# A transformer block in one program: the order of TensorE's three-product steps and of some small products

## The chip, the cores and the metric

The program runs on one core of a Trainium2 chip. The metric is the device time of one execution in microseconds (us); the time given for a kernel is the median of several executions. A profile is one execution of its own, with a start and a duration for every instruction of TensorE (PE, matmuls; PEld, the loads of their stationary operands), VectorE (DVE), ScalarE (ACT), GpSimd (POOL) and SyncE (SP, which issues most transfers).

## What is computed

One block of a hybrid network on a sequence of 1024 positions with 1024 features, all float32. `h` is normalised and multiplied by one wide matrix; three kinds of mixing work on slices of the result, and a gated merge and a feed-forward part follow:

```python
h = _rms(x, norm_mix_g[i])
proj = h @ w_in[i]                                  # 1024 x 8224
p_nsa, p_rwkv, p_gdn, p_gate = jnp.split(proj, ...)
o_a = _nsa(...)      # attention: compressed, selected and window keys
o_b, v_first = _rwkv7(...)                          # a recurrence with 8 heads of 64
o_c = _gdn(...)      # gated delta rule in chunks, 4 heads of 128
merged = gate0 * (o_a @ w_branch0) + gate1 * (o_b @ w_branch1) + gate2 * (o_c @ w_branch2)
x = x + merged @ w_out[i]
h = _rms(x, norm_ffn_g[i])
x = x + jnp.square(jax.nn.relu(h @ w_ff1[i])) @ w_ff2[i]
```

## The kernel before

**Dense steps.** The five large matrix products (`w_in`, three times `w_branch`, `w_out`, `w_ff1`, `w_ff2`) are done in a split form. Each float32 operand is held as a high part and a low part (`split`, L256 on): ScalarE casts the raw tile to the high part (`whi`, L259), and GpSimd or VectorE subtracts it from the raw tile to get the low part (`wlo`, L264), so the low part of a weight is always written last. One dense step is then three products of 128x128 by 128x512 into the same PSUM tile `fps`: high by high, high by low, low by high. There are 2368 such steps (7104 products). `mm3_steps` holds the loop for `w_in`; `tail` holds four more copies of the three lines, one for each later matrix.

**Small steps.** The three mixings are chains of small products with VectorE, ScalarE and GpSimd between them. They write PSUM tiles named `mps`. Some fill the whole 128x128 array (transposes against `ident`; `gZ,KQ`; the products of `PH` and `PL`, the high and low part of attention weights, with `V2s` and `V2w`); others use only 64 or 32 of its rows or columns (`xs,U`, `VS,AG`, `wa,up`, and `PH` or `PL` with `V2c`, the compressed values, which have 64 rows). A row of the profile shows that as 128\*128, 64\*128 and so on.

**What sets the order.** The code is written as generators. `run` steps the small chains, and between them takes single dense steps (`dense_step`) as filler, a share of TensorE's time that `BESIDE`, `GBESIDE` and `NBESIDE` set. The order in which the instructions then stand on each engine is chosen when the program is built: every instruction carries a priority number, `tc.cur_priority` at the time it was written, and dense steps are written with a number raised by 78, 100 or 1000 (`self.delta`), so that small steps that are ready go first. The built order is fixed; on the chip each engine goes through its own list, and an instruction waits on semaphores for operands from other engines. Before the change each of the three products of a dense step is placed by itself.

**The stages**, by the time in the profile before: the norm and the first columns of `w_in` (0 to 150 us), the recurrence `rwkv` with filler (150 to 630), `gdn` with filler (630 to 1050), the preparation of attention (1050 to 1160), attention with filler, from the middle on the first half of the tail (1160 to 1700), then the rest of the tail, which is dense steps almost alone (1700 to the end, with a seam between its two halves from 2000 to 2137).

Weights of `w_in` come in tiles of 512 rows by 128 columns, with two buffers for the raw tile and two for the parts (`FRAW`, `FBUF`); their low part is made on GpSimd alone (`FDIV`).

## Time and profile before

| | |
|---|---|
| median of 3 executions | 2495.28 us (2484.92 to 2502.08) |
| profiled execution | 2491.57 us, of which span of the profile 2489.5 us |
| instructions | 37131, of them 13589 matmul records |
| TensorE busy | 2357.2 us (95% of the span) |
| VectorE, ScalarE, GpSimd busy | 1396.8, 1060.3, 965.8 us |
| mean granted clock of TensorE | 0.974 |

A matmul's busy time in the profile includes what overlaps with the next one: a dense product has a duration of 390 to 430 ns, and the next one starts 0.23 us after it. The cost of a product is therefore read from the distance between two starts, not from its duration. The granted clock is a share of 2.4 GHz; it has two levels here, 1.0 and 0.5.

### The profile page before, as it was taken

To read this page: it belongs to the slowest core of one execution; us is meant where nothing else is said; L and a number is where in the kernel's file an instruction comes from. 1 tells how busy PE (TensorE), PEld (TensorE's weight loads), DVE (VectorE), ACT (ScalarE), POOL (GpSimd) and SP (SyncE) were. 2 spreads that over 40 slices of the span, in tenths; PEclk is the share of its full clock that TensorE was granted. 3 is DMA by queue.
4 is the path that set the end of the run, shared out by engine and by line. 5 is a ranking of instruction groups with operands and counts; after the bars stand their busy time and mean duration, and the time that the engine had idled before them with its cause. 6 is when DMAs were issued, how large, how long until landed. Compare 5 with 4: busy or idle time off the path is not lost.

```text
span 2489.5 us, 37131 instructions
## 1 busy us (share of the span) xinstructions
PE 2357.2 (95%) x13589; PEld 1891.7 (76%) x13589; DVE 1396.8 (56%) x3139; ACT 1060.3 (43%) x2101; POOL 965.8 (39%) x967
## 2 busy tenths in 40 slices
PE   6989999999899899899999999899999989999999
PEld 4767777777777778687887778788888867788887
DVE  4366766662675765223557787775444446545444
ACT  5454443322443433235667675654323334423231
POOL 4434444333221211235446684353333346233332
PEclk9989899999999999899999999999999999999999
DMA  4222223222223212552214331014323354223232
GB/s 139 69 64 64 59 66 76 68 72 69 69 55 84 53 49 80 146 114 73 62 56 135 97 110 42 21 62 138 101 94 95 109 181 145 82 89 110 85 110 93
DMA packets 319718, 216.79 MB, mean 87 GB/s; under 512 B 78486, under 2 KB 273184, under 8 KB 319536
## 3 DMA queue, kind: packets, MB, share of 16 engines
q1 hardware_dynamic: 308672, 195.63, 27.5%
q10 hardware_dynamic: 9792, 17.83, 2.0%
q8 instruction: 107, 1.75, 0.3%
q0 software_dynamic: 1072, 0.96, 0.2%
q14 instruction: 75, 0.61, 0.1%
HBM read 178.16 MB, written 36.22 MB: 86 GB/s over the span
## 4 chain that ended last, share of the span: by engine, by line
PE 77%; DVE 10%; DMA 5%; ACT 4%; issue 2%; POOL 1%; SPq 1%; ACTq 0%; DVEq 0%; POOLq 0%
PE fps L97 57%; PE mps L97 16%; PE mps L101 4%; DVE inv_p L341 2%; DVE inv_u L343 1%; DMA cw<-in_nsa_cmp_w_dram 1%; DVE gacc L895 1%; DMA lb<-inv 1%; DMA wraw<-in_w_branch_dram 1%; ACT P L1362 1%; DMA inv<-LT 1%; DVE ast L1357 1%; POOL wlo L264 0%; ACT whi L259 0%; DVE ast L1360 0%
## 5 line engine op out<-in xcount | busy, mean ns | idle before, releaser
L264 POOL TENSOR_TENSOR wlo<-wraw,whi 128x512 fp32r<-128x512 f32 (+2 forms) x408 | 525.1, 1289 | 907.1 <-ACT whi L259 877.9
L259 ACT CAST whi<-wraw 128x512 fp32r<-128x512 f32 (+1 forms) x408 | 286.6, 704 | 635.9 <-PE fps L97 430.6
L97 PE MATMUL fps<-hTh,whi 128*128 128x512 f32 x1024 | 442.5, 434 | 10.5 <-DVE wa L439 7.5
L97 PE MATMUL fps<-hTl,whi 128*128 128x512 f32 x1024 | 414.8, 407 | 0.0
L97 PE MATMUL fps<-hTh,wlo 128*128 128x512 f32 x1024 | 413.3, 408 | 1.3 <-POOL wlo L264 1.2
L264 DVE TENSOR_TENSOR wlo<-wraw,whi 128x256 fp32r<-128x256 f32 (+1 forms) x207 | 131.5, 638 | 224.6 <-ACT whi L259 219.3
L97 PEld LDWEIGHTS fps<-hTh,whi 128*128 128x128 f32 x1024 | 198.9, 195 | 52.3 <-DVE wa L439 7.6
L97 PEld LDWEIGHTS fps<-hTh,wlo 128*128 128x128 f32 x1024 | 198.3, 194 | 47.2 <-POOL wlo L264 2.7
L97 PEld LDWEIGHTS fps<-hTl,whi 128*128 128x128 f32 x1024 | 199.7, 195 | 32.5 <-issue 0.3
L97 PE MATMUL fps<-h2h,whi 128*128 128x512 f32 x512 | 200.0, 391 | 1.3 <-DVE h2l L296 1.3
L1376 POOL TENSOR_SCALAR P<-P,ast 128x64 f32<-128x64 f32 (+5 forms) x128 | 137.9, 1094 | 161.6 <-DVE ast L1369 96.1
L97 PE MATMUL fps<-h2l,whi 128*128 128x512 f32 x512 | 199.5, 390 | 0.0
L97 PE MATMUL fps<-h2h,wlo 128*128 128x512 f32 x512 | 199.3, 390 | 0.0
L97 PE MATMUL fps<-whi,fl 128*128 128x512 f32 x512 | 191.0, 389 | 0.0
L97 PE MATMUL fps<-whi,fh 128*128 128x512 f32 x512 | 189.9, 391 | 0.0
L97 PE MATMUL fps<-wlo,fh 128*128 128x512 f32 x512 | 189.0, 389 | 0.0
L1455 DVE TENSOR_TENSOR acc<-fps,acc 128x512 f32<-128x512 f32 x160 | 106.8, 686 | 105.8 <-PE fps L97 105.5
L1362 ACT ACTIVATE P<-mps,ast 128x128 f32<-128x128 f32 (+4 forms) x256 | 125.1, 494 | 72.5 <-DVE ast L1360 42.4
L1357 DVE TENSOR_REDUCE ast<-mps 128x1 f32<-128x128 f32 (+4 forms) x256 | 109.0, 442 | 56.6 <-PE mps L97 53.8
L1405 DVE TENSOR_TENSOR PL<-mps,PH 128x512 fp32r<-128x512 f32 (+2 forms) x168 | 103.3, 620 | 48.8 <-ACT PH L1404 48.1
L1404 ACT CAST PH<-mps 128x512 fp32r<-128x512 f32 (+2 forms) x168 | 88.2, 534 | 64.9 <-PE mps L101 59.4
L97 PEld LDWEIGHTS fps<-h2h,whi 128*128 128x128 f32 x512 | 96.2, 188 | 21.4 <-DVE h2l L296 1.8
(468 smaller groups left out, 4696.6 us busy)
## 6 DMA issues: line engine op xcount, KB each, us to landing
wraw<-in_w_in_dram SPq DMA_DIRECT2D x152, 256.0 KB, 2.9
wraw<-in_w_ff_dram SPq DMA_DIRECT2D x128, 256.0 KB, 2.8
wraw<-in_w_ff_dram SPq DMA_DIRECT2D x64, 512.0 KB, 3.4
gates<-fst ACTq DMA_DIRECT2D x48, 256.0 KB, 2.0
wraw<-in_w_branch_dram SPq DMA_DIRECT2D x48, 256.0 KB, 3.1
gin<-gates SPq DMA_DIRECT2D x48, 256.0 KB, 3.0
wraw<-in_w_out_dram SPq DMA_DIRECT2D x16, 512.0 KB, 3.4
nsa_in<-fst ACTq DMA_DIRECT2D x20, 256.0 KB, 2.1
```

What stands on the lines that cost most here:

```text
L97: return self.note(self.nc.tensor.matmul(out, lhsT=lhsT, rhs=rhs, **kw))
L101: return self.note(self.nc.tensor.transpose(out, x, ident))
L259: nc.scalar.copy(hi, raw)
L264: eng.tensor_tensor(out=lo[:, x], in0=raw[:, x], in1=hi[:, x].bitcast(F32), op=OP.subtract)
L341: nc.vector.tensor_tensor(out=v, in0=lt[:n, s, None, s + 1:].to_broadcast([n, w, w]), in1=u[:n, s + 1:, s + 1:].rearrange("p t c -> p c t" ...
L343: nc.vector.tensor_reduce(out=u[:n, s, s + 1:], in_=v, axis=AX, op=OP.add)
L1357: nc.vector.tensor_reduce(out=(mx if i == 0 else mx2)[:, b:b + 1], in_=ps[:, :n], axis=AX, op=OP.max, negate=True)
L1362: nc.scalar.activation(out=Pt[:, c:c + n], in_=tiles[i][:, :n], func=AF.Exp, bias=mx[:, b:b + 1], accum_out=(sm if i == 0 else sm2)[:, b:b ...
L1376: eng.tensor_scalar(out=Pt[:, c:c + n], in0=Pt[:, c:c + n], scalar1=r[:, b:b + 1], scalar2=None, op0=OP.mult)
L1404: nc.scalar.copy(PH[:n, x0:x1], ps[:n, x0:x1])
L1405: tt(out=PL[:n, x0:x1], in0=ps[:n, x0:x1], in1=PH[:n, x0:x1].bitcast(F32), op=OP.subtract)
L1455: tt(out=acc[:, st, c0:c0 + 512], in0=ps, in1=acc[:, st, c0:c0 + 512], op=OP.add)
```

## The change

Two things change, both only on TensorE. First, a dense step is written by a new helper `three`: the product with the low part of the weights comes first, and the second and third are written with a priority number 4000 lower, so that they stand right behind the first. Second, in four places small products are written in another order: the one whose operand is written last comes first (`rk` before `sq`; the heads in reversed order in two loops of the recurrence; `PL` before `PH`). No product, operand or buffer is added or taken away.

```diff
@@ mm3_steps
-            self.te.matmul(ps, lhsT=wh[:, k, m], rhs=rh[:, kk, n], start=(kk == 0), stop=False)
-            self.te.matmul(ps, lhsT=wh[:, k, m], rhs=rl[:, kk, n], start=False, stop=False)
-            self.te.matmul(ps, lhsT=wl[:, k, m], rhs=rh[:, kk, n], start=False, stop=(kk == (kts or kt) - 1))
+            self.three(ps, (wl[:, k, m], rh[:, kk, n]), (wh[:, k, m], rh[:, kk, n]), (wh[:, k, m], rl[:, kk, n]),
+                       kk == 0, kk == (kts or kt) - 1)
             yield
+    def three(self, ps, a, b, c, start, stop):
+        self.te.matmul(ps, lhsT=a[0], rhs=a[1], start=start, stop=False)
+        at = self.tc.cur_priority
+        self.tc.cur_priority = max(0, at - 4000)
+        self.te.matmul(ps, lhsT=b[0], rhs=b[1], start=False, stop=False)
+        self.te.matmul(ps, lhsT=c[0], rhs=c[1], start=False, stop=stop)
+        self.tc.cur_priority = at
@@ _rwkv_unit
+            self.te.matmul(ps[:, 8 + 2 * i:10 + 2 * i], lhsT=rk[:, two], rhs=sums[:, 2 * pp + i // 2], start=True, stop=True)
             self.te.matmul(ps[:, 2 * i:2 * i + 2], lhsT=sq[:, two], rhs=sums[:, 4], start=True, stop=True)
-            self.te.matmul(ps[:, 8 + 2 * i:10 + 2 * i], lhsT=rk[:, two], rhs=sums[:, 2 * pp + i // 2], start=True, stop=True)
...
-            for x, h, o in heads:
+            for x, h, o in reversed(heads):
                 self.te.matmul(pv[o, 0, x], lhsT=ag[:, x, h], rhs=vs[:, x, h], start=True, stop=True)
...
-            for x, h, o in heads:
+            for x, h, o in reversed(heads):
                 self.te.matmul(pv[o, 2, x], lhsT=kb[:, x, h], rhs=vs[:, x, h], start=True, stop=True)
@@ _pv_mm
-            self.te.matmul(po, lhsT=v, rhs=PH[:n, x], start=(b0 + j == 0), stop=False)
-            self.te.matmul(po, lhsT=v, rhs=PL[:n, x], start=False, stop=(b0 + j == last))
+            self.te.matmul(po, lhsT=v, rhs=PL[:n, x], start=(b0 + j == 0), stop=False)
+            self.te.matmul(po, lhsT=v, rhs=PH[:n, x], start=False, stop=(b0 + j == last))
@@ tail (w_out and w_ff2; w_branch and w_ff1 in the same way)
-                        self.te.matmul(ps, lhsT=lhs[0](k0 + k)[:, m], rhs=wh[:, j, :], start=(k == 0), stop=False)
-                        self.te.matmul(ps, lhsT=lhs[0](k0 + k)[:, m], rhs=wl[:, j, :], start=False, stop=False)
-                        self.te.matmul(ps, lhsT=lhs[1](k0 + k)[:, m], rhs=wh[:, j, :], start=False, stop=(k == 3))
+                        hi, lo = (t(k0 + k)[:, m] for t in lhs)
+                        self.three(ps, (hi, wl[:, j, :]), (hi, wh[:, j, :]), (lo, wh[:, j, :]), k == 0, k == 3)
```

What that does to the built order shows at two places. The first is TensorE in attention, at its third unit of queries and heads (`ident,P` transposes the attention weights, `PH` and `PL` are their parts, `K2c` the compressed keys, `fps` a dense product). Before:

```order
L97 MATMUL mps<-PH,V2w 128x256
L97 MATMUL mps<-PL,V2w 128x256
L101 MATMUL mps<-ident,P 128x128 x4
L97 MATMUL fps<-hTh,whi 128x512
L97 MATMUL fps<-hTl,whi 128x512
L97 MATMUL fps<-hTh,wlo 128x512
L97 MATMUL mps<-PH,V2c 128x256
L97 MATMUL fps<-hTh,whi 128x512
L97 MATMUL mps<-PL,V2c 128x256
L101 MATMUL mps<-ident,P 128x128 x4
```

The same place in the changed kernel:

```order
L97 MATMUL mps<-K2c,QL 128x64
L97 LDWEIGHTS identb
L97 MATMUL mps<-mcmp,identb 128x64
L97 MATMUL fps<-hTh,wlo 128x512
L97 MATMUL fps<-hTh,whi 128x512
L97 MATMUL fps<-hTl,whi 128x512
L97 MATMUL mps<-PL,V2c 128x256
L97 MATMUL mps<-PH,V2c 128x256
L101 MATMUL mps<-ident,P 128x128 x4
```

The two products with `V2c` had a dense product between them and now stand together, behind a whole dense step.

The second place is TensorE early in the recurrence, where one PSUM tile of dense steps, `fps_561`, gives way to the next, `fps_660` (the names carry their buffer numbers here; `gd,upg` is a small product that fills the array). Before:

```order
L97 MATMUL fps_561<-hTh_132,wlo_595 128x512
L97 MATMUL fps_660<-hTh_132,whi_663 128x512
L97 MATMUL fps_660<-hTl_133,whi_663 128x512
L97 MATMUL mps_1853<-gd_490,upg_1670 128x256 x2
L97 MATMUL fps_660<-hTh_132,wlo_664 128x512
```

The same place in the changed kernel:

```order
L97 MATMUL fps_561<-hTh_132,wlo_595 128x512
L97 MATMUL fps_561<-hTh_132,whi_594 128x512
L97 MATMUL fps_561<-hTl_133,whi_594 128x512
L97 MATMUL mps_1853<-gd_490,upg_1670 128x256 x2
L97 MATMUL fps_660<-hTh_132,wlo_664 128x512
```

The small products stood between the second and the third product of the first step of `fps_660`; now they stand between two whole steps.

Counted over TensorE's whole list: of 2368 dense steps 175 had small products among their three before, and 12 have now; 284 had products of another dense step among them, and 44 have now. Small products come in 598 groups between dense products before, in 514 now. The part of the array that a product uses (128\*128, 64\*128, 128\*64, 64\*64, 32\*32) changes from one product to the next 706 times before, 618 times now. The two products of each `V2c` pair stand apart in 25 of 32 cases before, in none now. The first product of a dense step carries 481 semaphore waits before and 751 now, the second 183 and 246, the third 419 and 59; small products carry 1734 and 1666.

## Rows read from the trace of the kernel before

**Rows 1.** The page's busy times: busy us, share of span, count.

```profile
PE 2357.2 (95%) x13589; PEld 1891.7 (76%) x13589; DVE 1396.8 (56%) x3139; ACT 1060.3 (43%) x2101; POOL 965.8 (39%) x967
```

**Rows 2.** Windows by stage: stretch, length, busy us and count by engine, clock.

```profile
1160.00:1610.00 450.00, 432.49 (x2520) 353.22 (x2520) 310.56 (x748) 296.93 (x767) 252.76 (x212) 0.98 0.24 74
150.00:630.00 480.00, 460.11 (x3850) 345.11 (x3849) 285.44 (x799) 177.26 (x325) 181.47 (x218) 0.95 0.27 68
630.00:1050.00 420.00, 382.02 (x2264) 312.37 (x2262) 257.77 (x690) 156.87 (x260) 95.77 (x110) 0.96 0.27 74
...
1700.00:2000.00 300.00, 300.00 (x1335) 248.56 (x1333) 145.79 (x197) 95.64 (x144) 102.24 (x86) 1.00 0.33 108
```

**Rows 3.** The page's chain of waits that ended last, share by engine.

```profile
PE 77%; DVE 10%; DMA 5%; ACT 4%; issue 2%; POOL 1%; SPq 1%; ACTq 0%; DVEq 0%; POOLq 0%
```

**Rows 4.** Timeline of PE, attention: start, us, instruction; a pair apart.

```profile
1173.49 0.40 PE L97 MATMUL fps<-hTh,wlo 128*128 128x512 f32 x1
1173.81 0.38 PE L97 MATMUL mps<-PH,V2c 64*128 64x256 f32 x1
1174.12 0.50 PE L97 MATMUL fps<-hTh,whi 128*128 128x512 f32 x1
1174.56 0.38 PE L97 MATMUL mps<-PL,V2c 64*128 64x256 f32 x1
1174.87 0.66 PE L101 MATMUL mps<-ident,P 128*128 128x128 f32 x4
```

**Rows 5.** Timeline of PE, attention, a pair together.

```profile
1219.30 0.28 PE L97 MATMUL mps<-PH,V2w 128*128 128x256 f32 x1
1219.41 0.28 PE L97 MATMUL mps<-PL,V2w 128*128 128x256 f32 x1
1219.63 0.38 PE L97 MATMUL mps<-PH,V2c 64*128 64x256 f32 x1
1219.85 0.28 PE L97 MATMUL mps<-PL,V2c 64*128 64x256 f32 x1
1220.06 0.44 PE L101 MATMUL mps<-ident,P 128*128 128x128 f32 x2
```

**Rows 6.** Timeline of PE, recurrence: dense products behind small ones on part of the array.

```profile
406.94 0.45 PE L97 MATMUL mps<-xs,U 64*64 64x64 f32 x8
407.31 0.50 PE L97 MATMUL fps<-hTh,whi 128*128 128x512 f32 x1
407.65 0.39 PE L97 MATMUL fps<-hTl,whi 128*128 128x512 f32 x1
407.88 0.40 PE L97 MATMUL fps<-hTh,wlo 128*128 128x512 f32 x1
```

**Rows 7.** Timeline of PE, recurrence: a dense product before whole-array transposes.

```profile
164.58 0.39 PE L97 MATMUL fps<-hTh,wlo 128*128 128x512 f32 x1
164.81 0.60 PE L101 MATMUL mps<-ident,BK 128*128 128x128 f32 x4
```

**Rows 8.** PE's waits, 150 to 1700 us: waiter, awaited, us in total, times, longest.

```profile
PE mps L97 <- DVE VS L712: 7.8, 10, 2.1
PE mps L97 <- ACT P L1362: 7.6, 12, 1.7
```

**Rows 9.** PE's waits over the whole span; columns as in rows 8.

```profile
PE fps L97 <- ACT whi L259: 4.9, 5, 1.8
...
PE fps L97 <- POOL wlo L264: 1.2, 2, 0.6
```

**Rows 10.** Groups by form: busy us, mean ns, then idle us before and its releasers.

```profile
L264 POOL TENSOR_TENSOR wlo<-wraw,whi 128x512 fp32r<-128x512 f32 x257 | 366.5, 1427 | 594.0 <-ACT whi L259 575.1 <-PE mps L97 10.3 <-PE fps L97 4.6
L259 ACT CAST whi<-wraw 128x512 fp32r<-128x512 f32 x328 | 202.8, 620 | 516.7 <-PE fps L97 353.3 <-DMA wraw<-in_w_ff_dram 55.9 <-issue 36.1
```

**Rows 11.** Windows in late attention; columns as in rows 2, clock third from last.

```profile
1590.60:1600.80 10.20, 9.40 (x40) 8.51 (x41) 6.05 (x16) 10.03 (x23) 0.04 (x1) 0.50 0.03 7
1576.00:1590.60 14.60, 10.93 (x69) 8.50 (x67) 10.16 (x27) 11.05 (x27) 7.93 (x6) 1.00 0.13 37
```

More of the change, by code (lines that the diff above doesn't have):

```diff
@@ L1477, in tail @@
                             for k in range(4):
-                                self.te.matmul(ps, lhsT=wh[:, k], rhs=oh[k], start=(k == 0), stop=False)
-                                self.te.matmul(ps, lhsT=wh[:, k], rhs=ol[k], start=False, stop=False)
-                                self.te.matmul(ps, lhsT=wl[:, k], rhs=oh[k], start=False, stop=(k == 3))
+                                self.three(ps, (wl[:, k], oh[k]), (wh[:, k], oh[k]), (wh[:, k], ol[k]), k == 0, k == 3)
                                 yield
@@ L1509, in up @@
                                 k = kh * 4 + j
-                                self.te.matmul(ps, lhsT=wh[:, j], rhs=h2[0][:, k], start=(k == 0), stop=False)
-                                self.te.matmul(ps, lhsT=wh[:, j], rhs=h2[1][:, k], start=False, stop=False)
-                                self.te.matmul(ps, lhsT=wl[:, j], rhs=h2[0][:, k], start=False, stop=(k == KT - 1))
+                                self.three(ps, (wl[:, j], h2[0][:, k]), (wh[:, j], h2[0][:, k]), (wh[:, j], h2[1][:, k]),
+                                           k == 0, k == KT - 1)
                                 yield
```

## The prediction

> **What bounds the kernel now.** I read the busy times first, then the windows by stage, then the chain of waits, and last the timeline of TensorE at the places that the change touches. The busy times put TensorE far ahead: 2357.2 us of the 2489.5 us span [rows 1]. So 2489.5 - 2357.2 = 132.3 us of the span are open gaps on it. The windows say where: from 1700 to 2000 us there is no gap at all and the clock is at its upper level, 2.4 GHz; in the recurrence the gaps are 480 - 460.1 = 19.9 us, in `gdn` 420 - 382.0 = 38.0 us, in attention 450 - 432.5 = 17.5 us [rows 2], together 75.4 us. The chain that ended last agrees: 77% of it is TensorE, 10% VectorE [rows 3]. So the time is TensorE's own work plus its gaps, and a change that only moves TensorE's instructions can do three things: make the same work take less between two starts, close gaps, or open others. The dense tail, where nothing stands between dense steps, can give nothing: there one product follows another and no order of the three changes their number.
>
> A busy TensorE is read by distances between starts. A dense product behind a dense product takes 0.23 us (407.65 to 407.88) [rows 6].
>
> **The change part by part.**
>
> *Pairs with the compressed values.* A product that uses 64 of 128 rows costs more at its edges. In [rows 4] the dense product before `PH,V2c` lasts from 1173.49 to 1173.81, 0.32 us instead of 0.23; `PH,V2c` takes 0.31; the dense product between the two takes 0.44 (1174.12 to 1174.56); `PL,V2c` takes 0.31. From 1173.49 to 1174.87 that is 1.38 us, and without two dense products at 0.23 it is 0.92 us. Where the two stand together [rows 5], the product before them takes 0.22 instead of the 0.11 of its like, an extra of 0.11, and they take 0.22 and 0.21: 0.54 us. The difference is 0.38 us a pair, and 25 of 32 pairs are brought together. All 25 would give 9.5 us; where the neighbours of an apart pair are themselves on part of the array, one edge is saved instead of two, which I bound by half, 4.8 us. Most apart pairs stand between full-size products as in [rows 4], so I take 8 us.
>
> *Other edges.* The used part of the array changes 88 times less often. The 25 pairs hold two changes each, 50; 38 are left. An edge into part of the array costs 0.32 - 0.23 = 0.09 us (1173.49 to 1173.81) [rows 4], an edge back costs 0.34 - 0.23 = 0.11 us (407.31 to 407.65) [rows 6]. 38 x 0.10 = 3.8 us; bounds 3.4 and 4.2. The other groups that disappear go between full-size products, where the dense product before whole-array transposes takes its normal 0.23 us (164.58 to 164.81) [rows 7]: no price, so none of the 598 - 514 = 84 vanished groups is counted for itself.
>
> *Whole steps before small ones.* 175 - 12 = 163 dense steps no longer let small products in between their three. At each of these places one or two dense products, 0.23 or 0.45 us, now run before the small product, whose operands have that much longer to come. What TensorE waited there shrinks; what it did not wait is unchanged. The two largest kinds of waits of small products hold 22 waits and 15.4 us [rows 8]. If 175 of 598 groups, 0.29, hold the same share of waits, 6 of the 22 shrink by a mean 0.34 us, 2 us; scaled from 15.4 to the 75.4 us of gaps it is 10 us. But many other gaps are single waits at the start of a stage that no third of a microsecond closes, so I take 4 us, bounds 2 and 10.
>
> *The low part first.* The lead of a dense step now waits for `wlo`, which takes GpSimd 1.43 us behind the cast to `whi` [rows 10]; before, two products (0.45 us) ran in that time. Where TensorE already waited for `whi`, 5 times and 4.9 us in all [rows 9], the wait grows, by up to 5 x (1.43 - 0.45) = 4.9 us; the low end is 0, where a small step's end decides in any case. ScalarE, GpSimd and VectorE get no more to do, but the weight tile's high part is released one product (0.23 us) later and its low part is needed two products (0.45 us) earlier: the cycle of release, cast, subtraction and lead loses 0.68 us of slack at each load of `w_in`. It stays hidden as long as the load in the other buffer, at least twelve products or 2.7 us, outlasts cast and subtraction, 0.62 + 1.43 = 2.05 us [rows 10]. TensorE waited for `wlo` only 1.2 us in all [rows 9], so there is slack, thin where there is little small work. I take a loss of 3 us.
>
> *Reversed heads, `rk` before `sq`.* The same products on the same parts of the array; one wait on the last operand in place of two, the first of which ended while the second was still pending. I take 0; at most 0.1 us for each of 64 places in either direction if the chain through them ends last.
>
> *The clock.* From 1590.6 to 1600.8 us the granted clock was at 0.50, that is 1.2 GHz, although TensorE was busy for 9.40 of 10.2 us with transposes and small products; just before it had been at 2.4 GHz, with gaps of 14.60 - 10.93 = 3.7 us in the 14.6 us that went ahead [rows 11]. [...]
>
> The sum: -8 - 3.8 - 4 + 3 = -12.8 us on the profiled execution's 2491.57 us, 2478.8 us. That execution lay 3.7 us below the median 2495.28 us of the runs shown, so the forecast for a median is 2482 us, half a per cent faster. With all bounds at their ends it is -24 to -5 us, 2471 to 2490 us.
>
> **The rivals.**
>
> *The gaps close much more.* With whole steps as units the built order might fit the chip better everywhere. If a third of the 75.4 us of gaps went, 25 us, with the edges (12) and the loss (3), the change would be -34 us: 2461 us. For it: 163 places get more cover, and small products carry 68 semaphore waits less. Against it: the gaps that have names in [rows 8] are few, and the number of dense products between a small step's last link and its next looks much the same in both orders.
>
> *Small chains held back, the slower side.* In `gdn` and in the recurrence each link of a chain goes from TensorE to VectorE and back. A link that finds a dense step begun now waits 0.23 or 0.45 us. As long as filler is left, TensorE loses nothing, since it works in that time; from the point on where a stage ends with its chain and not with its filler, every such wait counts. `gdn` has the widest gaps, 38.0 us [rows 2], which speaks for it. 163 places x 0.34 us = 55 us if all of them were on the path; with half of them 28 - 12 + 3 = +19 us: 2514 us. Against it: 77% of the chain is TensorE's own work [rows 3], and 84 + 11 of the 175 places lie in attention and behind it, where two streams and the tail's filler stand in.
>
> *The clock.* If the longer stretches without dense products cost two more low stretches like that of [rows 11], each of 10.2 us at half the clock, 5 us apiece, the sum becomes -3 us: 2492 us.
>
> *The edges are worth nothing.* If a chain through the other engines ends each mixed stage, the 12 us saved on TensorE become wider gaps: 2494 us. Against it stands a TensorE that is 91 to 96% busy in these stages [rows 2].
>
> That the change does not do what it says is excluded by the built order: 2312 of 2368 steps stand whole, 1909 before.
>
> **How the numbers follow.** Forecast 0.48, gaps close much more 0.25, chains held back 0.13, clock 0.07, edges worth nothing 0.07. About 1%, 25 us, is what a measurement of this kernel can tell from no change (the three runs shown spread over 17 us). Faster than 2470 us: most of the first rival (0.22) and the lower end of the forecast (0.07), 0.29. Slower than 2520 us: the part of the second rival in which more than half of the places count, and what I have not thought of, 0.10. Within 1%: 0.61. The range goes from 2452 us, which takes in most of the first rival, to 2512 us, which takes in the forecast with its bounds, the clock and nearly half of the slower rival; some 0.1 is left out on either side.
>
> **What would show it.** In the changed kernel's timeline the two products with `V2c` should follow each other at 0.22 us, their shorter one with a duration of 0.28 us in all 32 pairs. Dense products between 1700 and 2000 us should still follow at 0.23 us. The waits of TensorE on `wlo` should grow from a little over 1 us to 3 to 8 us, those on `whi` vanish. The open gaps of the three stages should fall from 75 us to about 70. I am wrong if gaps in `gdn` and the recurrence grow together by more than 15 us (chains held back), if the mean clock falls below 0.965 (clock), if the gaps fall by more than 20 us (first rival), or if the waits on `wlo` go beyond 15 us because the two buffers of `w_in` no longer cover cast and subtraction.

## The result and the profile after

The changed kernel takes 2523.16 us (median of 4 runs, 2521.57 to 2528.11), the kernel before 2495.58 us in the same comparison (4 runs, 2484.92 to 2502.08): ratio 1.0116, 95% interval 1.0093 to 1.014 (the ratio is a kernel's time over that of the kernel before; above 1 is slower). That is 27.6 us slower, where 13 us faster was forecast, and outside the range.

The first lines of the page of the changed kernel, with TensorE's busy time [rows 1], and the mean granted clock of its profiled run:

```profile
span 2526.4 us, 37034 instructions
PE 2364.9 (94%) x13589; PEld 1903.5 (75%) x13589; DVE 1406.8 (56%) x3139; ACT 1061.5 (42%) x2102; POOL 963.7 (38%) x967
...
core 0: 2526.4 us, clock 0.963
```

The span grew by 2526.4 - 2489.5 = 36.9 us, TensorE's busy time by 7.7 us. That is some 9 us more than the medians differ by: the profiled execution of the changed kernel was the slowest of its four, and that of the kernel before lay 4 us under its median. Where the time went, the windows by stage tell. The stages are cut at the same products in both kernels: the recurrence up to the last transpose of `Y`, `gdn` up to that of `gO`, the preparation, attention up to the last `V2c` product, and the tail. First the kernel before, then the changed one; columns are the stretch, its length, busy time (and instructions) of TensorE, of its weight loads and of the other engines, then the granted clock:

```profile
64.50:608.30 543.80, 521.65 (x4156) 391.47 (x4156) 324.31 (x892) 213.02 (x398) 213.34 (x230) 0.96 0.27 67
608.30:1031.80 423.50, 391.70 (x2313) 320.54 (x2311) 261.23 (x694) 159.43 (x264) 96.47 (x115) 0.97 0.25 67
1031.80:1135.30 103.50, 91.63 (x440) 75.69 (x438) 22.40 (x53) 31.71 (x57) 33.55 (x50) 0.92 0.60 142
1135.30:1707.40 572.10, 549.95 (x3177) 450.09 (x3176) 384.33 (x914) 364.15 (x933) 314.06 (x260) 0.98 0.23 72
1707.40:2484.70 777.30, 761.13 (x3336) 625.32 (x3336) 377.76 (x519) 256.08 (x387) 281.29 (x233) 0.99 0.35 112
```

```profile
65.00:618.80 553.80, 522.61 (x4157) 393.05 (x4157) 330.75 (x892) 212.21 (x398) 213.52 (x230) 0.95 0.26 66
618.80:1064.60 445.80, 405.29 (x2311) 332.37 (x2311) 263.48 (x694) 157.50 (x263) 98.51 (x115) 0.93 0.23 63
1064.60:1170.30 105.70, 94.74 (x454) 78.07 (x452) 22.63 (x53) 34.16 (x61) 35.60 (x51) 0.94 0.60 144
1170.30:1737.00 566.70, 536.14 (x3165) 443.69 (x3164) 383.97 (x914) 364.08 (x931) 311.01 (x258) 0.98 0.23 71
1737.00:2521.60 784.60, 764.15 (x3336) 627.57 (x3336) 378.66 (x519) 257.53 (x387) 278.77 (x233) 0.99 0.35 111
```

`gdn` lost most: +22.3 us with the same products. Its open gaps went from 423.5 - 391.7 = 31.8 to 445.8 - 405.3 = 40.5 us, +8.7; the other 13.6 us are busy time of the same work, and the granted clock beside it fell from 0.97 to 0.93. The recurrence lost 10.0 us, 9.0 of it gaps; the tail 7.3; attention gained 5.4: its busy time fell by 13.8 us, and 8.4 us of that came back as gaps. Over the span the mean clock went from 0.974 to 0.963; the speed that was not granted is 2489.5 x 0.026 = 64.7 us before and 2526.4 x 0.037 = 93.5 us after, +28.8 us (part of that is idle time: inside the span some 17 of the 131 us at 0.50 before and 25 of the 188 us after are gaps of TensorE). The clock of the traces is a share of full speed, 1.00 or 0.50 at any time; where 2.4 and 1.2 GHz are named in the texts on record, these two levels are meant, and no run shows a frequency.

What was meant to happen on TensorE did happen. The two products with `V2c`, by tile (count, then duration in ns: shortest, median, longest), first the second of a pair before, then both after: now the second has the short duration in 31 of the 32 pairs, median 276 ns, as forecast (the one left, 417 ns, ran at a granted clock of 0.50):

```profile
L97 PE MATMUL mps<-PL,V2c x32: 271/380/579, 1159.3 to 1707.4; 64*128 64x256 f32 x32
```

```profile
L97 PE MATMUL mps<-PL,V2c x32: 380/383/579, 1189.7 to 1736.8; 64*128 64x256 f32 x32
L97 PE MATMUL mps<-PH,V2c x32: 271/276/417, 1190.0 to 1737.0; 64*128 64x256 f32 x32
```

Dense products between 1740 and 2000 us still start 0.227 us apart in the median, before and after, as forecast.

TensorE's waits over the span of the changed kernel (us in total, times, longest), those that answer to [rows 8, 9]:

```profile
PE mps L97 <- ACT P L1372: 13.5, 14, 2.7
PE fps L97 <- ACT oh L259: 11.7, 3, 5.3
PE mps L97 <- DVE VS L722: 10.1, 11, 2.7
...
PE mps L101 <- ACT gv L906: 8.4, 4, 3.1
...
PE fps L97 <- DVE wlo L264: 3.8, 4, 1.9
PE fps L97 <- POOL wlo L264: 2.2, 3, 1.4
```

The waits for `wlo` came to 6.0 us, inside the forecast 3 to 8, and those for `whi` are gone. Only the 2.2 us for GpSimd's `wlo` are in steps of `w_in`, all before 140 us; the 3.8 us for VectorE's are in the tail. In `gdn` there is none of either. What grew there are waits of the small chain, `gv` above all. In the kernel before, the waits for `gv`, and those for VectorE's `wlo`, which [rows 9] does not show, were:

```profile
PE mps L101 <- ACT gv L896: 3.7, 2, 2.9
...
PE fps L97 <- DVE wlo L264: 1.1, 1, 1.1
```

So the waits for `whi` and `wlo` together were 4.9 + 1.2 + 1.1 = 7.2 us before and are 6.0 us now.

Two places show how. The first is in `gdn`, TensorE before (start, duration, instruction, in brackets the wait just ahead and what ended it):

```profile
677.09 0.63 PE L101 MATMUL mps<-ident,gv 128*128 128x128 f32 x4 [1.61 <-DVE inv_u L343]
...
678.73 0.66 PE L101 MATMUL mps<-ident,KQ 128*128 128x128 f32 x4 [0.29 <-DVE gVn L1008]
```

and the same place after, with a dense product behind it:

```profile
687.74 0.63 PE L101 MATMUL mps<-ident,gv 128*128 128x128 f32 x4 [1.45 <-DVE gkn L997]
...
692.09 1.12 PE L101 MATMUL mps<-ident,KQ 128*128 128x128 f32 x4 [3.02 <-DVE gVn L1018]
...
693.43 0.63 PE L97 MATMUL fps<-hTh,whi 128*128 128x512 f32 x1
693.86 0.63 PE L97 MATMUL fps<-hTl,whi 128*128 128x512 f32 x1
```

With equally many dense products between, the wait for `gVn` grew from 0.29 to 3.02 us, and behind it dense products start 0.43 us apart instead of 0.23: the granted clock is 0.50 from 692.9 to 696.3 us. `gVn` needs `gkn`, a square root on ScalarE. ScalarE at this place, before:

```profile
675.32 0.62 ACT L259 CAST whi<-wraw 128x512 fp32r<-128x512 f32 x1 [3.26 <-PE fps L97]
675.85 0.58 ACT L886 COPY graw<-fps 128x512 f32<-128x512 f32 x1
676.45 1.28 ACT L997 ACT_TABLE_LOAD   x1
677.74 0.21 ACT L997 ACTIVATE gkn<-gkn 128x4 f32<-128x4 f32 x1
```

and after:

```profile
686.32 0.58 ACT L896 COPY graw<-fps 128x512 f32<-128x512 f32 x1 [3.91 <-PE fps L97]
686.80 0.62 ACT L259 CAST whi<-wraw 128x512 fp32r<-128x512 f32 x1
687.45 1.28 ACT L924 ACT_TABLE_LOAD   x1
688.74 1.06 ACT L924 ACTIVATE zs<-graw 128x1024 f32<-128x1024 f32 x1
689.81 1.28 ACT L1007 ACT_TABLE_LOAD   x1
691.11 0.20 ACT L1007 ACTIVATE gkn<-gkn 128x4 f32<-128x4 f32 x1
```

In the built order of ScalarE the copy of `graw` and the cast of `whi` have changed places, and the gate's `zs`, which needs that copy, now stands ahead of `gkn` with a table load of its own: 2.3 us that the chain waits for. No line of the diff speaks of ScalarE.

The second place is at the turn from the tail of the first half to that of the second. SyncE's queue, before and after (start, time until the last of the group is issued):

```profile
1980.70 1.42 SPq L1465 DMA_DIRECT2D or<-o_a  x3
2000.34 2.87 SPq L1533 DMA_DIRECT2D out_dram<-acc  x4
```

```profile
2027.02 1.04 SPq L1539 DMA_DIRECT2D out_dram<-acc  x2
2028.11 2.31 SPq L1474 DMA_DIRECT2D or<-o_a  x3
```

The loads `or`, from which the second half's `oh` is cast, were issued 20 us ahead of the stores of the first half's result; now they stand behind two of these, which wait for the last sums in `acc`. TensorE's first wait at this turn grew from 1.1 us (for `ol`) to 5.3 us (for `oh`). That is about what the gaps of the whole tail grew by, from 16.2 to 20.4 us.

### The profile page after: what moved, and what is told of

Same layout as the page of the kernel before. It is cut to its first block, busy times and chain, and to the rows that moved or that the text cites. A ratio compares the mean times of both kernels' runs of the same rounds, so it can differ in the third digit from the quotient of the medians.

```text
span 2526.4 us, 37034 instructions
## 1 busy us (share of the span) xinstructions
PE 2364.9 (94%) x13589; PEld 1903.5 (75%) x13589; DVE 1406.8 (56%) x3139; ACT 1061.5 (42%) x2102; POOL 963.7 (38%) x967
## 4 chain that ended last, share of the span: by engine, by line
PE 51%; DMA 4%; DVE 3%; ACT 2%; issue 1%; POOL 1%; SPq 0%; ACTq 0%; POOLq 0%; DVEq 0%
PE fps L97 41%; PE mps L97 7%; PE mps L101 2%; DMA wraw<-in_w_branch_dram 1%; DMA cw<-in_nsa_cmp_w_dram 1%; ACT P L1372 1%; DVE PL L1415 1%; ACT whi L259 0%; DVE ast L1367 0%; POOL wlo L264 0%; DMA wraw<-in_w_ff_dram 0%; DMA gates<-fst 0%; DVE ast L1375 0%; DMA or<-o_a 0%; DVE ast L1370 0%
## 5 line engine op out<-in xcount | busy, mean ns | idle before, releaser
L97 PE MATMUL fps<-hTh,wlo 128*128 128x512 f32 x1024 | 457.4, 447 | 10.2 <-DVE wa L448 7.6
L97 PE MATMUL fps<-hTh,whi 128*128 128x512 f32 x1024 | 416.0, 406 | 0.0
L97 PE MATMUL fps<-wlo,fh 128*128 128x512 f32 x512 | 200.8, 392 | 0.0
L97 PE MATMUL fps<-whi,fh 128*128 128x512 f32 x512 | 199.3, 389 | 0.0
L97 PE MATMUL fps<-whi,fl 128*128 128x512 f32 x512 | 199.2, 389 | 0.0
L97 PEld LDWEIGHTS fps<-h2h,wlo 128*128 128x128 f32 x512 | 96.3, 188 | 20.2 <-DVE wlo L264 0.5
```

Source lines behind the costliest of these rows:

```text
L97: return self.note(self.nc.tensor.matmul(out, lhsT=lhsT, rhs=rhs, **kw))
```

## The experiments

The theories. T1: whole steps hold the small chains back. T2: the low part at the head costs, because it is needed earlier. T3: the edits in the small steps cost. T4: the clock falls behind waits and multiplies what they cost; it goes with any of the others. After twelve runs a fifth was added. T5: no cost belongs to an edit; each only makes ties in the built order of all engines fall otherwise, and the order of the kernel before is a good one among many. Each kernel was timed beside the kernel before on the same chip. "Longer" of a stage speaks of one profiled run each. How far chance goes there, stages with the same built order show: the two profiles of one kernel (`best_all`, `best_again`) differ by up to 2.4 us in a stage, the recurrences of `lowfirst_only` and `lf_zs` by 4.5 us. Over the whole, 23 executions of the kernel before went from 2483.75 us at a mean clock of 0.978 to 2506.9 us at 0.966. The diffs are shortened; `..` and bare pairs of names stand for the operands.

**The edits one by one.** `group_only`: three together, in the old order inside.

```diff
-            self.te.matmul(ps, lhsT=wh.., rhs=rh..); self.te.matmul(ps, lhsT=wh.., rhs=rl..); self.te.matmul(ps, lhsT=wl.., rhs=rh..)
+            self.three(ps, (wh.., rh..), (wh.., rl..), (wl.., rh..), ...)     # in all dense steps
```

> The dense step's three products stay together (second and third at the raised priority), but in the old order: high by high, high by activations' low part, weights' low part last. Nothing else is changed. Theory 1, whole steps hold the chains of gdn and the recurrence back: this kernel carries the loss, 30 to 38 us over the kernel before (its gain at the V2c pairs is absent), with gdn and the recurrence together longer by about 30 us. Theory 2, the low part at the head: this kernel is within 8 us of the kernel before. Theory 3, the small steps' new order: within 8 us as well. Theory 4, the clock falls after gaps and doubles what they cost: it goes with theory 1 or 2, and the time at 1.2 GHz, 133 us before and 190 us after, rises wherever the loss is, by about twice the loss.

Measured: 2502.41 us, ratio 1.0029 (1.0011 to 1.0047), +8.6 us. `gdn` took 424.1 us (423.4 before), the recurrence 537.1 (543.8), attention 578.9 (572.1), the tail 784.4 (777.3). The chains of `gdn` and the recurrence are not held back; T1 fails as it was put, and what grouping loses lies in attention and the tail.

`lowfirst_only`: the order of the change in all dense steps, without the raised priority, and the small steps as before. The diff is against the change.

```diff
     def three(self, ps, a, b, c, start, stop):
-        self.tc.cur_priority = max(0, at - 4000)
+        self.tc.cur_priority = at
```

> The product with the weights' low part leads each dense step, but no priority is raised, so that small products may stand between the three as before. Theory 2: this kernel carries the loss, 25 to 38 us over the kernel before, and TensorE's waits for the low part grow from about 1 us to several. Theory 1: 0 to 5 us over the kernel before. Theory 3: the same as before within 8 us.

Measured: 2516.38 us, ratio 1.0092 (1.0056 to 1.0129), +22.5 us. It carries the loss; `gdn` 435.7 us, recurrence 553.1. But TensorE's waits for `wlo` were 7.9 us in the whole span and none in `gdn`.

`small_only`: `PL` ahead of `PH`, reversed heads, `rk` ahead of `sq`; dense steps as before.

```diff
-            self.te.matmul(po, lhsT=v, rhs=PH[:n, x], start=(b0 + j == 0), stop=False)
-            self.te.matmul(po, lhsT=v, rhs=PL[:n, x], start=False, stop=(b0 + j == last))
+            self.te.matmul(po, lhsT=v, rhs=PL[:n, x], start=(b0 + j == 0), stop=False)
+            self.te.matmul(po, lhsT=v, rhs=PH[:n, x], start=False, stop=(b0 + j == last))
```

> Only the edits in the small steps: the low half of the attention weights ahead of the high half with each block of compressed values, the two reversed loops over heads, rk ahead of sq. Dense products as in the kernel before. Theories 1 and 2: 5 to 10 us below the kernel before, all of it in attention, by the V2c pairs that now stand together. Theory 3: 15 to 35 us over the kernel before, lost in the recurrence and gdn.

Measured: 2490.75 us, ratio 0.9982 (0.9962 to 1.0002), -3.1 us. 30 of the 32 pairs have the short second product (median 277 ns; the other two ran at 0.50, 417 ns at the longest), attention took 567.3 us (572.1), but the recurrence 551.0 (543.8). T3 falls.

`dense_both`: the change without the edits in the small steps.

> Both edits of the dense steps (three together, low part first), without the edits in the small steps. Theory 1 and theory 2: 30 to 38 us over the kernel before, 5 to 10 us over the whole change, which has the V2c pairs together. Theory 3: within 8 us of the kernel before. If neither of the two alone carries the loss but both together do, the causes multiply: a chain that is held back by grouped steps which themselves wait for the low part.

Measured: 2525.65 us, ratio 1.0127 (1.0088 to 1.0165), +31.8 us. The two parts add: 22.5 + 8.6 = 31.1. With the small edits, 31.1 - 3.1 = 28.0 us against 27.6 measured of the whole change. That they meet so closely is luck, as each interval reaches 4 to 10 us to either side.

**Where the low part loses.** `act_low` changes the order without touching the low part's place.

```diff
-  (wh, rh), (wh, rl), (wl, rh)
+  (wh, rl), (wh, rh), (wl, rh)     # steps of w_in
```

> The order inside the dense steps of w_in is changed to high by activations' low part, high by high, weights' low part last: the products move, but the weights' low part keeps its place, and the built order of the other engines stays as in the kernel before but for a few rows. If the order of the three products itself costs something (weights loaded anew, accumulation), 10 to 22 us over the kernel before. If the loss of the low part at the head comes from the time at which it is needed, or from what that does to the built order of the other engines, within 5 us of the kernel before.

Measured: 2497.23 us, ratio 0.9999 (0.9978 to 1.0019). The order of three products costs nothing by itself; the built orders of ScalarE and VectorE stayed nearly as they were.

`low_gdn` and `low_notgdn` put the low part first in one stage or in the others (the branch on the filler's share, which is 0.5 in `gdn` alone).

```diff
+            if self.share == 0.5:  (wl, rh), (wh, rh), (wh, rl)   # low_gdn; low_notgdn has the two branches exchanged
+            else:                  (wh, rh), (wh, rl), (wl, rh)
```

> Low part first only in the steps of w_in that are built during gdn. In its built order ScalarE has the gate's activation zs ahead of the second square root gkn once, as in every kernel with the low part first there. If the loss sits in gdn by its own built order: gdn 8 to 15 us longer than before, the whole 8 to 18 us over the kernel before. If gdn only suffers from a shift that begins in the opening or in the recurrence: within 5 us.

> The mirror: low part first in the opening, the recurrence, the preparation and attention, the old order in gdn and in the tail. zs and gkn stand as before on ScalarE. If the loss sits in gdn: gdn within 5 us of before, and the whole 0 to 12 us over it (what the recurrence loses). If the shift from the earlier stages does it: 18 to 25 us over the kernel before.

Measured: `low_gdn` 2511.59 us, ratio 1.0061 (1.0034 to 1.0089), with `gdn` at 438.3 us; `low_notgdn` 2503.07 us, ratio 1.0043 (1.0024 to 1.0062), with `gdn` at 425.9 and the recurrence at 555.0. Each stage loses where the low part is first, and 0.61 + 0.43 = 1.04% against the 0.92% (0.56 to 1.29) of `lowfirst_only`, which has it in both and in the tail.

`lf_zs` takes the low part first and undoes the swap on ScalarE.

```diff
+            self.tc.add_manual_dep(zs_ins, self.root.name, Tensor.EDGE, reason="gate behind the root")
```

> The kernel with the low part first everywhere, and one edge more, which keeps the gate's activation zs behind the square root gkn on ScalarE; its built order differs from that kernel's by four rows of ScalarE and by none of TensorE, VectorE or GpSimd. If the swap of zs and gkn is what costs gdn its time: at the place of the swap TensorE's two waits of 2.7 and 1.7 us shrink to 1.6 and 0.3 us as before, the clock does not fall there, and the kernel is 4 to 10 us faster than with the low part first alone. If the loss is spread over many places: 2 to 4 us.

Measured: 2516.57 us, ratio 1.0082 (1.0057 to 1.0107). The two waits shrank from 2.7 and 1.7 to 1.5 and 1.2 us, yet `gdn` took 434.6 us. At this place the clock fell all the same, behind the waits that were left, for 3.4 us in place of 6.8. The swap is one such place among several.

**Grouping in the tail.** `group_tail`: three together, old order, only behind attention.

```diff
-                        self.te.matmul(ps, lhsT=lhs[0](k0 + k)[:, m], rhs=wh[:, j, :], ..)    # tail; mm3_steps stays as before
-                        self.te.matmul(ps, lhsT=lhs[0](k0 + k)[:, m], rhs=wl[:, j, :], ..)
-                        self.te.matmul(ps, lhsT=lhs[1](k0 + k)[:, m], rhs=wh[:, j, :], ..)
+                        self.three(ps, (hi, wh[:, j, :]), (hi, wl[:, j, :]), (lo, wh[:, j, :]), ..)
```

> Three together in the old order, but only in the steps behind attention (output, branch weights, first feed-forward weights); the steps of w_in as before. If grouping loses in the dense tail, where the prediction gave it nothing: the stage behind the last V2c product 6 to 9 us longer than the 777 us before, with TensorE's first long wait there for oh growing from about 1 to over 4 us, and the whole 5 to 9 us over the kernel before. If grouping loses its time in the steps of w_in: within 4 us of the kernel before.

Measured: 2509.58 us, ratio 1.0044 (1.0025 to 1.0063), the tail at 783.7 us. TensorE's waits for `oh` at the turn, first the kernel before, then this one:

```profile
PE fps L97 <- ACT oh L259: 6.1, 2, 5.0
```

```profile
PE fps L97 <- ACT oh L259: 13.1, 3, 5.7
```

In its queue on SyncE three stores stand ahead of the loads `or`. Two or three do so in seven of the kernels here (the change, `group_only`, `group_tail`, `dense_both`, `no_low`, `jit_b`, `jit_d`), and their tails took 781.9 to 786.7 us; in all others the loads come first, and the tails took 776.6 to 780.6 us. `jit_b` and `jit_d` group nothing: the longer tail goes with the order on SyncE, and grouping is one way to that order. The order on SyncE was not put in alone.

**The cycle of the weight buffers.** `base_w3` gives `whi` a third buffer (and `xs` one instead of two, for the memory), `lf_w3` the same with the low part first.

```diff
-        hi = pool.tile([P, kt, cols], F32R, name="whi", tag="whi", bufs=bufs)
+        hi = pool.tile([P, kt, cols], F32R, name="whi", tag="whi", bufs=3 if pool is self.fpool else bufs)
```

> The kernel before with a third buffer for the weights' high part of w_in and one buffer less for xs, which pays for its memory. It is the measure for the next kernel. All theories: within 6 us of the kernel before.

> Low part first everywhere, with the third buffer for the high part, so that the cast for a load no longer waits for the load two before it and the 0.68 us of slack in the cycle of release, cast, subtraction and lead is given back many times over. If the lost slack of that cycle is the cause: within 6 us of the same kernel without the low part first. If it is the order that is built when the lead becomes ready later, whatever the buffers: 15 to 25 us over it, with zs ahead of gkn once in gdn as in its built order.

Measured: `base_w3` 2509.27 us, ratio 1.004 (1.002 to 1.006), `lf_w3` 2522.32 us, ratio 1.0089 (1.0055 to 1.0124). The difference, 13 us, lies between the two expectations, and the buffers alone cost 0.4%, 10 us, where at most 6 were expected: the first sign for T5. In `gdn` the low part first makes 429.3 - 424.1 = 5.2 us here, 435.7 - 423.4 = 12.3 us without the third buffer, and the waits for `gv` are 8.4 us in 4 waits all the same. So the buffer may take off a part, and not the pattern of the waits; on the slack as a whole it is inconclusive.

**Need, release, or reshuffle.** `lead_sync` keeps the old order but lets the lead wait for the subtraction, by a dependency.

```diff
             i = self.te.matmul(ps, lhsT=wh[:, k, m], rhs=rh[:, kk, n], start=(kk == 0), stop=False)
+            self.tc.add_manual_dep(i.ins, made, SYNC, reason="lead behind the low part")
```

> The old order of the three products, but the leading product of each step of w_in also waits for the subtraction that makes the weights' low part, as the lead does in the change. When the high part is released stays as before, and the built order of the other engines differs from before by 46 rows on ScalarE, against 662 with the low part first. If the lead's need of the low part costs the time, on TensorE or by the slack of its cycle: 12 to 22 us over the kernel before. If the reshuffled order of the other engines does: within 5 us of it.

Measured: 2502.89 us, ratio 1.0011 (0.9992 to 1.003). The need of the low part at the head, by itself, costs nothing that can be measured (by the interval at most 0.3%, 7 us): T2 falls as it was put.

`low_second`: `(wh, rh), (wl, rh), (wh, rl)` in the steps of `w_in`.

> The steps of w_in in the order high by high, weights' low part, high by activations' low part: the low part is needed one product earlier than before (two in the change) and the high part is released one product later, as in the change. Built order: 426 rows of ScalarE differ from before, with zs ahead of gkn once in gdn. If the reshuffle by the later release costs the time: 10 to 22 us over the kernel before, most of it in gdn and the recurrence. If the place of the low part at the head does: 0 to 8 us.

Measured: 2499.67 us, ratio 1.001 (0.9992 to 1.0029), which is what was expected of T2, but in `gdn` the waits of `lowfirst_only` came back one by one. The windows of `gdn` for `lowfirst_only`, `low_second`, `lead_sync`:

```profile
616.80:1052.50 435.70, 398.95 (x2312) 326.47 (x2311) 259.54 (x694) 157.36 (x263) 101.34 (x117) 0.95 0.24 65
```

```profile
612.30:1048.20 435.90, 399.40 (x2313) 327.27 (x2311) 260.82 (x694) 157.44 (x263) 100.73 (x119) 0.95 0.24 65
```

```profile
614.70:1037.60 422.90, 390.93 (x2311) 320.25 (x2311) 265.28 (x694) 159.55 (x264) 96.15 (x117) 0.97 0.25 67
```

So what costs in `gdn` comes with the later release of the high part, which both orders share, and not with the need at the head, which `lead_sync` has. The profiles of all kernels agree. In the seven that release the high part later during `gdn` (the change, `dense_both`, `lowfirst_only`, `lf_zs`, `low_gdn`, `low_second`, `lf_w3`), TensorE waits for `gv` 4 times, 8.0 to 8.4 us, and the stage took 434.6 to 445.8 us, 429.3 in `lf_w3` alone. In the eleven that do not, without the two that follow below, it waits twice, 3.6 to 3.7 us, and the stage took 422 to 426 us. For the whole this does not settle it: `low_second` has the longer `gdn`, in the recurrence and attention it took 549.3 and 569.5 us, and its interval ends at 0.3%. That the early need and the later release together use up a slack which each by itself leaves is not excluded.

`jit_b` and `jit_d`: the kernel before, with a fixed series added to each dense step's priority.

```diff
-        self.tc.cur_priority = at + self.delta
+        self.tc.cur_priority = at + self.delta + (self.count * 104729) % 9 - 4     # jit_d: (count * 1299709) % 25 - 12
```

> The kernel before with a small number from a fixed series, -4 to 4, added to the priority of each dense step. No product changes its place in its step for a reason of the computation; only ties in the built order fall otherwise (190 rows of ScalarE, 418 of VectorE), and zs stands ahead of gkn once in gdn, as with the low part first. If any reshuffle of the tuned order costs time: 5 to 20 us over the kernel before. If the low part first is a cause of its own: within 5 us of it.

> The same with another series, -12 to 12 (307 rows of ScalarE, 646 of VectorE, as many as with the low part first outside gdn); zs and gkn stand as before. If any reshuffle costs: 5 to 20 us over the kernel before, with more time at 1.2 GHz. If the low part first is a cause of its own: within 5 us.

Measured: `jit_b` 2530.92 us, ratio 1.0128 (1.0089 to 1.0166); `jit_d` 2510.17 us, ratio 1.0052 (1.0034 to 1.0071). Without one product in another place for a reason of the computation, `jit_b` loses as much as the whole change (the intervals overlap). Its windows of the recurrence and of `gdn`:

```profile
63.90:628.60 564.70, 540.96 (x4155) 403.64 (x4155) 328.77 (x892) 215.88 (x400) 214.16 (x228) 0.93 0.26 64
628.60:1061.50 432.90, 397.33 (x2311) 324.32 (x2310) 259.64 (x694) 159.53 (x264) 97.79 (x117) 0.95 0.24 66
```

The recurrence has no more gaps than before (564.7 - 541.0 = 23.7 us against 22.2) and yet is 20.9 us longer: its clock is 0.93 instead of 0.96. So the clock can fall without more waits, and other ties alone can cost as much as an edit, as T5 has it.

**What is left without the low part, and the best version.** `no_low` is the change with the old order inside `three`; `best_all` groups in `mm3_steps` alone, keeps the old order of the three and all edits in the small steps; `best_again` is the same kernel, timed longer.

```diff
-            self.three(ps, (wl.., rh..), (wh.., rh..), (wh.., rl..), ...)
+            self.three(ps, (wh.., rh..), (wh.., rl..), (wl.., rh..), ...)     # best_all: in mm3_steps only, tail as before
```

> The whole change but for the low part first: three together in the old order everywhere, with all edits in the small steps. If the parts add up as measured (grouping +7 us, small edits -4 to -5 us): 0 to 6 us over the kernel before, with the stage behind attention 6 to 9 us longer and attention shorter. If the low part first is not what carries the loss of the whole: 20 us or more.

> The version that the runs point to: three together in the old order in the steps of w_in, the dense steps of the tail as before, and all edits in the small steps. If grouping's loss is in the tail alone and the gains at the edges are real: 5 to 15 us under the kernel before. If grouping loses in the steps of w_in: within 5 us of it.

> The same kernel as best_all (three together in the steps of w_in alone, all small edits, old order of the three), timed in more rounds. If its gain is real: 4 to 10 us under the kernel before, interval without 1. If it was the chip's spread: an interval that holds 1.

Measured: `no_low` 2493.53 us, ratio 1.0002 (0.9986 to 1.0018), attention at 561.8 us, the tail at 781.9. `best_all` 2486.86 us, ratio 0.9971 (0.9949 to 0.9992); `best_again` 2490.58 us, ratio 0.9984 (0.9964 to 1.0004). By these ratios the best version is 4 to 7 us ahead of the kernel before and 33 to 36 us ahead of the change; that it beats the kernel before is likely, but the second interval still holds 1.

The change and `no_low` differ in the low part first alone, and the ratio goes from 1.0002 to 1.0116 with it. Three more pairs differ in just that: the kernel before and `lowfirst_only` (1 and 1.0092), `group_only` and `dense_both` (1.0029 and 1.0127), `base_w3` and `lf_w3` (1.004 and 1.0089). In all four the low part first is slower, by 0.5 to 1.1%. So T5 does not hold as it was put: this edit costs in every surrounding in which it was tried.

## Why the prediction was wrong, point by point

*Pairs with the compressed values, -8 us.* The mechanism was right, with all pairs together and the short duration (median 276 ns, 380 before). The term is seen by itself in `small_only`: TensorE's busy time in attention fell from 550.0 to 540.5 us, but gaps grew by 4.7 us and the stage is 4.8 us shorter, and as a whole the small edits measured -3.1 us (interval -9.5 to +0.5). In the change busy time there fell by 13.8 us, and gaps took back 8.4. The step took a saving on TensorE for one of the stage, which the rival "edges are worth nothing" had seen in part.

*Other edges, -3.8, and whole steps before small ones, -4.* Not found as a sum: grouping alone measured +8.6 us, and the version that groups the steps of `w_in` alone is not separable from the small edits by themselves (0.9971 and 0.9984 against 0.9982). And the gaps that whole steps were to close grew: in the recurrence, `gdn` and attention from 76.1 us to 87.7 us with grouping alone, and to 102.3 us with the change, where about 70 were forecast. The sentence that failed here is that the dense tail can give nothing because no order of the three changes their number. Inside the halves of the tail it held; but the tail lost 7 us, at the seam between them, where the built order with grouping has the loads `or` behind stores on SyncE. The queue of another engine was not looked at there.

*The low part first, +3.* This is the step that failed most: +22.5 us measured by itself, and 1.1% between `no_low` and the change. The waits that it priced did not grow: those for `whi` and `wlo` together went from 7.2 to 6.0 us (its "1.2 us in all" for `wlo` left out 1.1 us for VectorE's), and the need at the head, put in alone, cost nothing measurable (`lead_sync`). It failed where it took ScalarE, GpSimd and VectorE as unchanged because they get no more to do. They get the same work in another order: 662 rows of ScalarE stand elsewhere with the low part first, a few where the other two products are exchanged (`act_low`), which costs nothing. How many rows move sets no price: 426 in `low_second` made 1.8 us, 307 in `jit_d` 12.3 and 190 in `jit_b` 33.0 us. It matters which rows. Shown is that in `gdn` the longer stage and its waits for `gv` go with the later release of the high part, and one of its places (`zs` ahead of `gkn`), where the order of ScalarE made the wait; that this place alone isn't the loss is shown too (`lf_zs`).

*Reversed heads and `rk`, 0.* Not separated from the pairs; nothing speaks against 0.

*The clock, no term in the sum.* Wrong: over the span, the speed that was not granted grew by 28.8 us (0.974 to 0.963), most in `gdn`. In the recurrence it decides nearly alone: in the kernels run here the stage took 537.1 to 565.7 us, with 27 us at a clock of 0.50 in the shortest and 85 us in the longest (`group_only`, `lf_w3`), half of that difference being 29 us and the stages' 28.6; without half of its time at 0.50 the stage lies between 519 and 528 us in all of them. What makes the clock fall more often there is not shown. The rival on the clock had the sign and the sign to look for (a mean below 0.965), but no run shows its cause, that longer stretches without dense products lower the clock. The recurrence and `gdn` speak against it: `group_only` gathers the dense products and spent less time at 0.50 there than the kernel before, 51 against 72 us. In attention it spent more, 44 against 24 us, but so did `small_only`, 38 us, which gathers none; there the rival stays open.

*Small chains held back.* Its mark came true, gaps in `gdn` and the recurrence grew by 8.7 + 9.0 = 17.7 us, and its time, 2514 us, lay nearer than the forecast's. Its mechanism fell: grouping alone left `gdn` at 424.1 us and the recurrence at 537.1. That its time lay nearer is luck.

What stays open: which of the other rows in the built order cost the rest of `gdn`; why the recurrence spends more time at a clock of 0.50 in one order than in another; whether the change with the loads `or` kept ahead of the stores would have a tail of 778 us (that was not tried); and how far the slack of the weight buffers has a part (`lf_w3` was inconclusive, and `lead_sync` and `low_second` each take only a part of it).

## What to carry to other kernels

Where a scheduler builds the order, a change on one engine can be a change on all of them: compare the built order of every engine and of the DMA queues, not only that of the engine whose lines were edited, and follow each place where a row with a table load, or a load behind a store that waits, has moved ahead of a chain. And before a per cent is credited to an edit, run the old kernel with its ties broken otherwise: here that alone made 0.5 and 1.3%, as much as anything the edits did. An edit that seems worth keeping, like the pairs here, should then be tried alone, and its order chosen anew.

## What was not expected of the hardware

The granted clock also falls where TensorE is not waiting at all. The windows of the kernel before in the recurrence, and TensorE there, from just ahead of the fall:

```profile
262.00:266.00 4.00, 4.00 (x58) 3.19 (x57) 3.90 (x8) 2.53 (x5) 3.66 (x4) 1.00 0.45 112
266.00:270.00 4.00, 4.00 (x54) 3.50 (x52) 2.76 (x7) 2.04 (x3) 2.65 (x3) 0.96 0.24 66
270.00:275.00 5.00, 5.00 (x15) 3.01 (x15) 4.33 (x12) 0.97 (x3) 2.11 (x2) 0.50 0.20 52
275.00:280.00 5.00, 5.00 (x29) 3.69 (x28) 1.70 (x5) 0.65 (x2) 2.51 (x3) 0.50 0.01 3
```

```profile
266.29 0.93 PE L97 MATMUL mps<-AG,BK 64*128 64x128 f32 x6
...
268.59 1.15 PE L97 MATMUL mps<-L,U 64*64 64x64 f32 x32
269.66 0.59 PE L97 MATMUL mps<-sums,rk 128*128 128x2 f32 x2
```

TensorE is busy for all of it, at a clock of 1.00 up to 269.7 us and then at 0.50 for 17.1 us, after 3 us of small products: `AG,BK`, products with two columns, and `L,U`. The products with `ident` come later in the stretch, from 277 us on: this fall stands behind small products none of which is a transpose. In `gdn` of the changed kernel, on the other hand, the falls stand behind waits: in the 8 us ahead of each of the ten TensorE has 1.5 to 4.2 us of gaps, and in the 8 us ahead of 269.7 us above it has none. The one at 689.8 us falls inside the wait of 3.02 us, 2 us behind that of 1.45 us; both are waits for VectorE, and the dense products behind the second run at 0.50. So here a chain that a row on ScalarE held up by some 2 us was paid for twice, once as a wait (3.02 us in place of 0.29) and once as slower products behind it (0.43 us apart in place of 0.23).
